# Attention scores on one core: the 64-row products of four heads gathered behind the 128-row ones

## The chip, the cores and the metric

The kernel runs on one core of one Trainium2 chip. The metric is the device time of one execution in microseconds (us). Before the change it is 2775.07 us, the median of three runs (2773.48 to 2775.38).

## What is computed

The program is two transformer-like blocks, one after the other, for 256 tokens of width 2048 in float32. The first block is gated linear attention, a short convolution and a feed-forward layer; the second a pooling mixer and an attention layer with a shared latent for keys and values. The change lies in this last attention layer. It has 16 heads. A head's query and key have 192 entries, 128 of them without and 64 with a rotary position code. Queries come in blocks of 128, and a block sees the keys up to its own end, that is 128 keys for block 0 and 256 for block 1:

```python
QBLOCK, N_HEADS, QK_NOPE, QK_ROPE, QK_HEAD = 128, 16, 128, 64, 192

def chunk_causal_attention(q, k, v):
    S = q.shape[1]
    scale = QK_HEAD ** -0.5
    outs = []
    for i in range(S // QBLOCK):
        q0, k_end = i * QBLOCK, (i + 1) * QBLOCK
        s = jnp.einsum('bqhd,bkhd->bhqk', q[:, q0:k_end], k[:, :k_end],
                       preferred_element_type=jnp.float32) * scale
        q_chunk = (q0 + jnp.arange(QBLOCK)) // CHUNK
        k_chunk = jnp.arange(k_end) // CHUNK
        mask = k_chunk[None, :] <= q_chunk[:, None]
        s = jnp.where(mask[None, None], s, -1e30)
        p = jax.nn.softmax(s, axis=-1).astype(v.dtype)
        outs.append(jnp.einsum('bhqk,bkhd->bqhd', p, v[:, :k_end]))
    return jnp.concatenate(outs, axis=1)
```

The score of a head is therefore a sum over 192 entries, which the kernel forms as a product over 128 rows plus a product over 64 rows.

## The kernel before, in words

Nearly all of the time goes into products of activations with weights from device memory. A weight block of 1 MB is loaded by SyncE into a tile `raw`, and each half of it, a unit, is split into a high part `wh` (ScalarE, line 268) and a low part `wl` (VectorE, line 269), so that fast float32 products can add up to nearly full precision. There are three `raw` tiles and four pairs of `wh` and `wl`; a unit is split up to three units ahead of its use (`ensure`, lines 254 to 274). TensorE goes through the units in the order of `weight_order` (line 58).

The other work is written as generators. At the end of each unit (`end_unit`, line 324) every generator whose time has come is advanced to its next `yield`, unless the planned cost of VectorE or ScalarE is too far ahead of that of TensorE. The planned cost of a product is booked in `mm` (line 227), which also issues it. So the order of each engine's instructions is fixed when the program is built, and attention is spread between the units of the last weights (`MLA`, line 48).

The attention of four heads is one generator, `attend(hq)` (line 1306), four in all. Its parts in order:

- For each of the two blocks of queries (line 1325): take a `main` tile of PSUM with four places of 256 columns, one a head, and write the four heads' scores into it (lines 1329 to 1335). `qn` and `kn` hold the 128 entries without position code on 128 rows; `qr` and `krp` hold the 64 entries with it, and there two heads share a tile: the even head lies on rows 0 to 63, the odd one on rows 64 to 127 (`bs`, line 1332). `HEAD_AT = (0, 2, 1, 3)` says which head a place c has, so places 0 and 1 hold even heads and places 2 and 3 odd ones. A `start` flag at c = 0 and at c = 2 clears two places at a time; the other products accumulate.
- ScalarE copies the scores to `s` (line 1339), GpSimd writes -1e30 over the masked corner (line 1341).
- VectorE takes maxima (line 1349), ScalarE the exponentials (line 1359), VectorE divides by the sums (lines 1364 to 1367).
- TensorE transposes the probabilities (line 1374, twelve groups of four in all), ScalarE copies them to `pt`, and TensorE multiplies them with the values `v` (lines 1386 and 1387).

Everything in the score products is plain float32. Such a product appears in the trace as two passes, each a weight load (PEld) and a MATMUL (PE). A 64-row product is a pass of the form 64*128, a 128-row one of 128*128; with one block of queries it has 128 columns, with the other 256. There are 8 score blocks in the kernel (4 groups of heads, 2 blocks of queries), each with 4 products of either height.

Of the kernel before, what the change touches and what calls it, by code (L numbers as in the profile page):

```python
# [99 lines left out]
def kernel(  # L100
# [48 lines left out]
    def slot(name, shape=(P, 4, T), dt=F32):  # L149
        return Slot(spool, big_places, "slot", shape, dt, name)  # L150
# [22 lines left out]
    def psum_later(kind, shape):  # L173
        while len(psum_places[kind]) < (1 + state["spare"] if kind == "main" else 1):
            yield 1
        return Psum(kind, shape)
# [8 lines left out]
    def elems(a):  # L185
        return math.prod(a.shape[1:])
# [21 lines left out]
    def ts(out, a, s1, s2, op0, op1=None):  # L208
        vec_cost(out, 2.0)
        if op1 is None:  # L210
            nc.vector.tensor_scalar(out, a, s1, None, op0)
        else:
            nc.vector.tensor_scalar(out, a, s1, s2, op0, op1)
# [9 lines left out]
    def act(out, a, f, scale=1.0, bias=0.0, **kw):  # L223
        spent["ACT"] += elems(out) / 1.2 + 100
        nc.scalar.activation(out, a, f, bias=bias, scale=scale, **kw)  # L225

    def mm(out, lhsT, rhs, start, stop):
        n = elems(rhs)
        spent["PE"] += (n / 2.4 if rhs.dtype == F32R else max(n / 0.6, 214.0)) + 2
        nc.tensor.matmul(out, lhsT, rhs, start=start, stop=stop, skip_group_check=True)  # L230
# [188 lines left out]
    def group_tok(name, g, rhs, kbs=range(NKB)):  # L419

        ps = psum_now("main", (P, 2, 512))
        kbs = list(kbs)
        for i, kb in enumerate(kbs):
            for half in range(2):
                wh, wl = next_unit(name, g, kb)
                x = rhs(i)[half]
                for j in range(2):
                    first = i == 0 and half + j == 0
                    last = i == len(kbs) - 1 and half + j == 2
                    for t in range(2):  # L430
                        tk = slice(t * P, (t + 1) * P)
                        mm(ps[:, t, :], x[:, j, 0, tk], wh[:, j, :], first, False)
                        mm(ps[:, t, :], x[:, j, 0, tk], wl[:, j, :], False, False)
                        mm(ps[:, t, :], x[:, j, 1, tk], wh[:, j, :], False, last)
                end_unit()
        return ps
# [99 lines left out]
    def small(name, shape):  # L536
        return const.tile(list(shape), F32, name=uid(name))

    def rstd_steps(out, m, mean_plus_eps):

        mean_plus_eps()
        act(out, m, AF.Sqrt)
        yield 1
        recip(out, out)
        mul(m, m, out)
        mul(m, m, out)
        ts(m, m, -0.5, 1.5, ALU.mult, ALU.add)
        mul(out, out, m)
# [281 lines left out]
    for g in range(4):  # L830
        ps = group_tok("v", g, h)
# [4 lines left out]
    for g in range(4):  # L836
        hold = {}
        ps = group("cc", g, h)
# [6 lines left out]
        ps = group("cx", g, h)  # L845
# [19 lines left out]
        ps = group("cb", g, h)  # L865
# [12 lines left out]
    for g in range(4):  # L878
        ps = group("gb", g, h)
        gt = {}  # L880
        spawn(gate_steps(ps, get("R"), AF.Sigmoid, gt, 0))
        ps = group("conv_out", g, cbu)
# [11 lines left out]
    for g in range(4):  # L894
        ps = group("r", g, h)
# [15 lines left out]
    for g in range(4):  # L911
        ps = group("ga", g, h)
# [4 lines left out]
        ps = group("gla_out", g, op)  # L917
# [24 lines left out]
    def residual(g):  # L942
        def into(ps, fs):
            for part in range(2):
                add(xs[g][:, fs, :], ps[:, :, part, :], xs[g][:, fs, :])

        return into
# [77 lines left out]
    for part in range(4):  # L1025
# [5 lines left out]
        for g in range(4):  # L1031
            ps = group("down", g, hid, range(4 * part, 4 * part + 4), residual(g))
# [49 lines left out]
    for half in range(2):  # L1082
        y = Pair(4)
        for gi in (2 * half, 2 * half + 1):
            pooled = Pair(2)
            for n in range(2):
                ps = group("u", 2 * gi + n, hp)
# [5 lines left out]
            for n in range(2):  # L1093
                ps = group("pgate", 2 * gi + n, hp)
# [3 lines left out]
            for n in range(2):  # L1098
                ps = group("pgroup", 2 * gi + n, pooled, range(2))
# [15 lines left out]
        for g in range(4):  # L1115
            ps = group("pout", g, y, range(4 * half, 4 * half + 4), residual(g))
# [98 lines left out]
    kn, krp, vq = [None] * 4, [None] * 2, []  # L1215
# [45 lines left out]
    qn, qr, qr2 = [None] * 4, [None] * 2, [None] * 2  # L1261
# [43 lines left out]
    HEAD_AT = (0, 2, 1, 3)  # L1305
    def attend(hq):
        while None in (qn[hq], kn[hq], qr[hq // 2], krp[hq // 2]):
            yield 1
        while hq and (hq - 1 not in begun or state["unit"] < begun[hq - 1] + STAGGER):
            yield 1  # L1310
        while len(big_places) < 6:
            yield 1
        begun[hq] = state["unit"]

        rq = rows["Cq"]
        hs = slice(4 * hq, 4 * hq + 4)
        a, b = qss[:, :, hs], qsc[:, :, hs]
        for t in range(2):
            r = rq[:, t:t + 1]
            ts(qss[:, t, hs], qss[:, t, hs], r, r, ALU.mult, ALU.mult)  # L1320
        yield from rstd_steps(b, a, lambda: ts(a, a, 1.0 / QK_HEAD, EPS, ALU.mult, ALU.add))
        for t in range(2):
            ts(qsc[:, t, hs], qsc[:, t, hs], rq[:, t:t + 1], QK_HEAD**-0.5, ALU.mult, ALU.mult)
        probs, mxs = [], []
        for blk in range(2):
            w = P * (blk + 1)
            ps = yield from psum_later("main", (P, 4, T))
            qsl = slice(blk * P, (blk + 1) * P)
            for c in range(4):
                i = HEAD_AT[c]  # L1330
                hd = 4 * hq + i
                bs = slice(64 * (hd % 2), 64 * (hd % 2) + 64)
                jr = hd // 2
                mm(ps[:, c, 0:w], qn[hq][:, i, qsl], kn[hq][:, i, 0:w], c % 2 == 0, False)
                mm(ps[:, c, 0:w], qr[jr // 4][bs, jr % 4, qsl], krp[jr // 4][bs, jr % 4, 0:w], False, True)
            yield 1
            s = slot("s")
            probs.append(s)
            act(s[:, :, 0:w], ps[:, :, 0:w], AF.Copy)
            ps.done()  # L1340
            nc.gpsimd.memset(s[0:64, :, w - 64:w], -1e30)
        qn[hq].free()
        kn[hq].free()
        yield 1
        for blk in range(2):
            w = P * (blk + 1)
            mx = small("mx", (P, 3, 4))
            mxs.append(mx)
            nc.vector.reduce_max(mx[:, 0, :], probs[blk][:, :, 0:w], axis=AX.X)
            stt(mx[:, 0, :].rearrange("p (b a) -> p b a", b=2), mx[:, 0, :].rearrange("p (b a) -> p b a", b=2),  # L1350
                -1.0, qsc[:, blk, hs].rearrange("p (a b) -> p b a", b=2), ALU.mult, ALU.mult)
        yield 1
        for blk in range(2):
            w = P * (blk + 1)
            mx = mxs[blk]
            for c in range(4):
                hd = 4 * hq + HEAD_AT[c]
                sv = probs[blk][:, c, 0:w]
                act(sv, sv, AF.Exp, scale=qsc[:, blk, hd:hd + 1], bias=mx[:, 0, c:c + 1],
                    accum_out=mx[:, 1, c:c + 1])  # L1360
        yield 2
        for blk in range(2):
            w = P * (blk + 1)
            nc.vector.reciprocal(mxs[blk][:, 2, :], mxs[blk][:, 1, :])
            for c in range(4):
                sv = probs[blk][:, c, 0:w]
                ts(sv, sv, mxs[blk][:, 2, c:c + 1], None, ALU.mult)
        yield 2
        pt0, pt1 = slot("pt0"), slot("pt1", (P, 4, P))
        for src, sc, dst in ((probs[0], slice(0, P), pt0[:, :, 0:P]), (probs[1], slice(0, P), pt0[:, :, P:T]),  # L1370
                             (probs[1], slice(P, T), pt1.t)):
            ps = yield from psum_later("misc", (P, 4, P))
            for c in range(4):
                nc.tensor.transpose(ps[:, HEAD_AT[c], :], src[:, c, sc], ident)  # L1374
            yield 1
            act(dst, ps.t, AF.Copy)
            ps.done()
        for s in probs:
            s.free()
        yield 2  # L1380
        while len(vq) <= hq:
            yield 1
        po = yield from psum_later("main", (P, 4, T))
        for i in range(4):
            isl = slice(i * P, (i + 1) * P)
            mm(po[:, i, :], vq[hq][:, 0, isl], pt0[:, i, :], i % 2 == 0, False)
            mm(po[:, i, P:T], vq[hq][:, 1, isl], pt1[:, i, :], False, True)
        vq[hq].free()
        pt0.free()
        pt1.free()  # L1390
        yield 1
        o = slot("oraw")
        act(o.t, po.t, AF.Copy)
        po.done()
        while hq not in gates:
            yield 1
        yield 1
        mul(o.t, o.t, gates[hq].t)
        gates[hq].free()
        ob.put(hq, o.t)  # L1400
        o.free()

    for g in range(4):
        spawn(attend(g))
    uses = {"bgate": hb, "kvb_k": cl, "kvb_v": cl, "qb_r": ql, "qb_n": ql}
    for i, (name, g) in enumerate(MLA):
# [8 lines left out]
        else:  # L1415
            ps = group_tok(name, g, cl, [0])
# [134 lines left out]
```

## Time and profile before

| what | value |
|---|---|
| median of three runs | 2775.07 us |
| the profiled execution's own time | 2773.71 us |
| its span, first to last instruction | 2771.9 us |
| TensorE busy | 2759.3 us |
| VectorE busy | 1787.4 us |
| ScalarE busy | 1346.4 us |
| DMA, mean rate | 185 GB/s |
| first score block starts | 2560.46 us |
| last score product starts | 2628.9 us |

The span is counted from the first instruction. Busy times are those of the engine's own work; weight loads are counted apart from products and overlap them. The ends of products are modelled by the profile, so the distance between starts is the safer measure of a product's cost.

### The profile page before, as it was taken

The numbers are of one execution on the slowest core, as the hardware profiler recorded it, in microseconds if no ns is written. First come the engines' busy times: TensorE is split into PE (matmuls) and PEld (weight loads), VectorE is DVE, ScalarE is ACT, GpSimd is POOL, SyncE is SP. The second block draws the span as 40 slices with busy tenths as digits, with TensorE's granted clock in tenths as the row PEclk, the third lists the DMA queues.
The fourth block names the chain that finished last, engine by engine and source line by source line (L and its number), as shares of the span: only waits on it lengthen the run. The fifth ranks groups of instructions, "written<-read, shape, count | busy, mean of one in ns | idle before, by whom it ended". The sixth has DMA issues, their size and how long they took to land.

```text
span 2771.9 us, 38593 instructions
## 1 busy us (share of the span) xinstructions
PE 2759.3 (100%) x15906; PEld 2403.6 (87%) x15906; DVE 1787.4 (64%) x2119; ACT 1346.4 (49%) x1584; POOL 25.7 (1%) x36
## 2 busy tenths in 40 slices
PE   8999999999999999999999999999999999999999
PEld 7888888888888888888888888888888888899788
DVE  6676666655665666656556566687657677768464
ACT  5644444444554444434444345554434445555563
POOL 0000000000000000000000000000000000000000
PEclk9999999999999999999999999999999999999999
DMA  6444455555555655555555555555555555555244
GB/s 250 175 149 155 167 182 183 194 186 189 191 182 198 214 193 186 185 195 183 194 185 191 189 185 195 190 185 195 185 193 185 186 194 199 201 181 183 92 171 148
DMA packets 73712, 511.69 MB, mean 185 GB/s; under 512 B 8208, under 2 KB 8752, under 8 KB 13248
## 3 DMA queue, kind: packets, MB, share of 16 engines
q1 hardware_dynamic: 72496, 506.94, 51.9%
q8 instruction: 124, 2.03, 0.3%
q10 hardware_dynamic: 1040, 2.29, 0.2%
q14 instruction: 52, 0.43, 0.0%
HBM read 504.99 MB, written 4.21 MB: 184 GB/s over the span
## 4 chain that ended last, share of the span: by engine, by line
PE 99%; DVE 0%; DMA 0%; ACT 0%; issue 0%; SPq 0%; DVEq 0%; ACTq 0%
PE main L230 96%; PE misc L230 2%; DMA raw<-w_q_dram 0%; PE misc L1374 0%; DVE wl L193 0%; DVE cum L683 0%; ACT e L225 0%; ACT wh L225 0%; SPq L246 0%; ACT ls L225 0%; DVE x L193 0%; ACT L225 0%; DVE ls L206 0%; DVE out L193 0%; PE misc L1241 0%
## 5 line engine op out<-in xcount | busy, mean ns | idle before, releaser
L230 PE MATMUL main<-part,wh 128*128 128x512 f32 (+1 forms) x7360 | 2278.5, 392 | 6.9 <-ACT wh L225 6.9
L193 DVE TENSOR_TENSOR wl<-raw,wh 128x1024 fp32r<-128x1024 f32 (+1 forms) x946 | 1152.2, 1221 | 937.8 <-ACT wh L225 929.7
L230 PEld LDWEIGHTS main<-part,wl 128*128 128x128 f32 x7200 | 1354.4, 188 | 314.4 <-DVE wl L193 1.8
L225 ACT ACTIVATE wh<-raw 128x1024 fp32r<-128x1024 f32 (+1 forms) x946 | 997.3, 1058 | 1193.9 <-PE main L230 1100.1
L230 PE MATMUL main<-part,wl 128*128 128x256 f32 x7200 | 1430.2, 278 | 0.7 <-DVE wl L193 0.5
L230 PEld LDWEIGHTS main<-part,wh 128*128 128x128 f32 x7360 | 1124.0, 189 | 11.4 <-ACT wh L225 7.1
L193 DVE TENSOR_TENSOR out<-main,out 128x512 f32<-128x512 f32 x164 | 112.0, 684 | 8.3 <-ACT out L225 8.3
L230 PE MATMUL main<-wh,part 128*128 128x512 f32 x320 | 105.3, 400 | 0.0
L225 ACT ACTIVATE out<-main 128x512 f32<-128x512 f32 x164 | 94.6, 577 | 0.0
L193 DVE TENSOR_TENSOR x<-main,x 128x512 f32<-128x512 f32 x128 | 88.0, 688 | 9.9 <-PE main L230 7.7
L230 PEld LDWEIGHTS main<-wh,part 128*128 128x128 f32 x320 | 60.8, 190 | 12.8 <-issue 0.3
L230 PE MATMUL main<-wl,part 128*128 128x512 f32 x160 | 63.0, 394 | 0.0
L225 ACT ACTIVATE part<-out 128x512 fp32r<-128x512 f32 x56 | 33.2, 626 | 50.7 <-DVE out L206 44.2
L193 DVE TENSOR_TENSOR out<-out,R 128x1024 f32<-128x1024 f32 x42 | 51.4, 1225 | 1.3
L225 ACT ACTIVATE Z<-Z 128x1024 f32<-128x1024 f32 x16 | 17.0, 1061 | 42.0 <-DVE Z L193 36.9
L193 DVE TENSOR_TENSOR part<-out,part 128x512 fp32r<-128x512 f32 x56 | 36.2, 687 | 0.5
L230 PEld LDWEIGHTS main<-wl,part 128*128 128x128 f32 x160 | 30.6, 191 | 5.8
L225 ACT ACT_TABLE_LOAD x24 | 30.8, 1283 | 1.1 <-PEq L1540 0.7
L206 DVE SCALAR_TENSOR_TENSOR part<-x,vec,part 128x256 fp32r<-128x256 f32 x64 | 26.8, 478 | 5.3 <-ACT part L225 5.3
L1068 POOL COPY s<-out 128x4 f32<-128x4 f32 x8 | 9.5, 1187 | 2208.2 <-ACT wh L225 1809.7
L230 PEld LDWEIGHTS misc<-Z 128*128 128x128 f32 x240 | 29.0, 191 | 1.0
L230 PE MATMUL misc<-Z 128*128 128x64 f32 (+1 forms) x240 | 28.6, 271 | 0.0
(188 smaller groups left out, 824.4 us busy)
## 6 DMA issues: line engine op xcount, KB each, us to landing
raw<-w_up_dram SPq DMA_DIRECT2D x64, 1024.0 KB, 4.8
raw<-w_down_dram SPq DMA_DIRECT2D x64, 1024.0 KB, 4.8
raw<-w_u_dram SPq DMA_DIRECT2D x32, 1024.0 KB, 4.8
raw<-w_pgate_dram SPq DMA_DIRECT2D x32, 1024.0 KB, 4.8
raw<-w_pout_dram SPq DMA_DIRECT2D x32, 1024.0 KB, 4.8
raw<-w_v_dram SPq DMA_DIRECT2D x16, 1024.0 KB, 4.9
raw<-w_cc_dram SPq DMA_DIRECT2D x16, 1024.0 KB, 4.8
raw<-w_cx_dram SPq DMA_DIRECT2D x16, 1024.0 KB, 4.8
```

Source lines behind the costliest of these rows:

```text
L193: nc.vector.tensor_tensor(out, a, b, op)
L206: nc.vector.scalar_tensor_tensor(out, a, s, b, op0, op1)
L225: nc.scalar.activation(out, a, f, bias=bias, scale=scale, **kw)
L230: nc.tensor.matmul(out, lhsT, rhs, start=start, stop=stop, skip_group_check=True)
L1068: nc.gpsimd.tensor_copy(nx[:, :, 0:d], cur[:, :, 0:d])
```

## The change

Inside a block of queries the loop over the four places is split in two. The first loop issues the four 128-row products in the order of the places. The second issues the four 64-row products, in the order of places 0, 2, 1, 3, that is on rows 0 to 63, 64 to 127, 0 to 63, 64 to 127. Every product keeps its operands, its place and its flags.

```diff
             qsl = slice(blk * P, (blk + 1) * P)
             for c in range(4):
                 i = HEAD_AT[c]
-                hd = 4 * hq + i
+                mm(ps[:, c, 0:w], qn[hq][:, i, qsl], kn[hq][:, i, 0:w], c % 2 == 0, False)
+            for c in (0, 2, 1, 3):
+                hd = 4 * hq + HEAD_AT[c]
                 bs = slice(64 * (hd % 2), 64 * (hd % 2) + 64)
                 jr = hd // 2
-                mm(ps[:, c, 0:w], qn[hq][:, i, qsl], kn[hq][:, i, 0:w], c % 2 == 0, False)
                 mm(ps[:, c, 0:w], qr[jr // 4][bs, jr % 4, qsl], krp[jr // 4][bs, jr % 4, 0:w], False, True)
             yield 1
             s = slot("s")
```

## Rows read from the trace of the kernel before

**Rows 1.** The page: busy time and share by engine, and the chain that ended last.
```profile
PE 2759.3 (100%) x15906; PEld 2403.6 (87%) x15906; DVE 1787.4 (64%) x2119; ACT 1346.4 (49%) x1584; POOL 25.7 (1%) x36
...
PE 99%; DVE 0%; DMA 0%; ACT 0%; issue 0%; SPq 0%; DVEq 0%; ACTq 0%
```

**Rows 2.** Waits, 2555 to 2772 us: waiter, waited for, total us, times, longest.
```profile
DVE wl L193 <- ACT wh L225: 75.4, 46, 5.4
ACT wh L225 <- PE main L230: 50.4, 31, 3.3
...
PEld main L230 <- issue: 10.3, 31, 0.3
```

**Rows 3.** Timeline of PE, first score block: start us, duration us, work, passes merged.
```profile
2560.46 0.38 PE L230 MATMUL main<-kn,qn 128*128 128x128 f32 x2
2560.77 0.49 PE L230 MATMUL main<-krp,qr 64*128 64x128 f32 x2
2561.18 0.49 PE L230 MATMUL main<-kn,qn 128*128 128x128 f32 x2
...
2563.68 1.95 PE L230 MATMUL misc<-ones,sq 128*128 128x1 f32 x16
2565.49 0.49 PE L230 MATMUL main<-wh,part 128*128 128x512 f32 x1
```

**Rows 4.** Timeline of PE, second score block.
```profile
2572.67 0.59 PE L230 MATMUL main<-kn,qn 128*128 128x256 f32 x2
2573.19 0.70 PE L230 MATMUL main<-krp,qr 64*128 64x256 f32 x2
2573.82 0.70 PE L230 MATMUL main<-kn,qn 128*128 128x256 f32 x2
...
2577.58 0.38 PE L230 MATMUL misc<-ones,sq 128*128 128x1 f32 x2
```

**Rows 5.** The chain near 2617 us (start, us), then timeline of PE, value product.
```profile
2617.43 0.44 PE misc L1374 x4
...
2641.66 2.78 PE L230 MATMUL main<-pt,v 128*128 128x256 f32 x16
2644.28 0.60 PE L1374 MATMUL misc<-cm,s 128*128 128x128 f32 x4
```

**Rows 6.** All instructions that read krp: count, ns min/median/max, first and last start, forms.
```profile
L230 PEld LDWEIGHTS main<-krp,qr x64: 182/184/186, 2560.8 to 2628.7; 64*128 64x128 f32 x64
L230 PE MATMUL main<-krp,qr x64: 272/374/480, 2560.8 to 2628.9; 64*128 64x128 f32 x32, 64*128 64x256 f32 x32
```

**Rows 7.** Timeline, chain, and windows (us, engines' busy, granted clock, DMA share, GB/s).
```profile
2558.64 0.39 PE L230 MATMUL main<-wl,part 128*128 128x512 f32 x1
2559.32 0.39 PE L230 MATMUL main<-wl,part 128*128 128x512 f32 x1
...
2567.41 0.63 PE L230 MATMUL main<-wl,part 128*128 128x512 f32 x1
2568.69 0.63 PE L230 MATMUL main<-wl,part 128*128 128x512 f32 x1
...
2553.34 1.68 PE misc L230 x16
...
2567.00:2570.40 3.40, 3.40 (x10) 2.63 (x9) 0.00 (x0) 0.62 (x1) 0.00 (x0) 0.50 0.50 212
2580.60:2584.00 3.40, 3.40 (x12) 2.94 (x12) 0.00 (x0) 0.48 (x1) 0.00 (x0) 0.50 0.02 5
```

**Rows 8.** Timeline of VectorE's divided probabilities and of PE's transposes.
```profile
2639.49 1.14 DVE L211 TENSOR_SCALAR s<-s,mx 128x256 f32<-128x256 f32 x4
2649.17 1.14 DVE L211 TENSOR_SCALAR s<-s,mx 128x256 f32<-128x256 f32 x4
...
2647.52 0.60 PE L1374 MATMUL misc<-cm,s 128*128 128x128 f32 x4
2656.61 1.04 PE L1374 MATMUL misc<-cm,s 128*128 128x128 f32 x8
```

## The prediction

> **What bounds the kernel now.** I began with the page's busy shares and its chain of waits [rows 1]: TensorE is busy for 2759.3 of 2771.9 us and the chain that ends last runs on it for 99%. So a microsecond taken from TensorE's own stream is a microsecond of the kernel, as long as nothing else becomes late. Then the view of waits, for the stretch from the first score block to the end [rows 2]: no row has TensorE's products waiting for ScalarE, VectorE or a transfer. ScalarE, which makes the weights' high halves, instead waits 50.4 us for TensorE to free buffers; the producers run ahead. The 10.3 us under "issue" is a weight load starting late with nothing released, 31 times at up to 0.3 us: TensorE holding itself up.
>
> The timeline shows where. In the first score block (128 keys) the 128-row products (kn,qn) and the 64-row ones (krp,qr) alternate, two passes each [rows 3]. The seven pairs from 2560.77 to 2563.68 take 0.416 us each; the block lasts from 2560.46 to 2563.68, 3.22 us. In the second block (256 keys) the seven pairs from 2573.19 to 2577.58 take 0.627 us each and the block lasts 4.91 us [rows 4]. Compare f32 passes that follow each other without a change of height: four 128-column transposes advance the chain by 0.44 us, 0.11 us a pass, and sixteen passes of the value product, eight of 256 columns and eight of 128, take 2.62 us up to the next start [rows 5], which leaves (2.62 - 8 x 0.11) / 8 = 0.217 us for a pass of 256. So a pair should take 0.22 or 0.434 us and takes 0.416 or 0.627: **each change between 128 and 64 rows costs 0.195 us**, the same at either width. That is the shape of a fixed pause (finish the old products, then load weights in the open), not of slower streaming. It adds up: 16 x 0.11 + 7 x 0.195 = 3.13 of the 3.22 us, and 16 x 0.217 + 7 x 0.195 = 4.84 of the 4.91; the rest belongs to the change at the block's end, which stays.
>
> **The change, part by part.** Nothing is added or removed: the same 64 + 64 passes, the same operands, no DMA, no wait. No instruction of another engine moves, and the queues of SyncE and GpSimd are not touched. The planner's estimate for a block is the same sum of the same calls, so the order around it stays.
>
> *Changes of height.* A block has eight now: seven inside it and one at its end. With the four 128-row products first there are two, one inside and one at the end. Six go, in each of 4 x 2 = 8 blocks (the 64-row products have 32 passes of either width [rows 6], eight to a block): 48 x 0.195 = **9.4 us**. Both widths pay the same, so no split is needed. All of it lies on TensorE's stream.
>
> *Changes of half.* The 64-row products now follow each other on rows 0 to 63, 64 to 127, 0 to 63, 64 to 127: three changes of half in a block, 24 in all. The trace of before has no such neighbours, so the price is bounded. Upper end: as dear as a change of height, 24 x 0.195 = 4.7 us given back. Lower end: the two halves run beside each other, and at each change one pass hides behind the one before. With 256 columns that hides 0.217 us three times in four blocks, 2.6 us. With 128 columns it need not hide anything: sixteen one-column passes take 2565.49 - 2563.68 = 1.81 us, 0.113 each [rows 3], so 0.11 us is what a weight load takes with nothing to stream; if loads overlap too it is up to 3 x 4 x 0.11 = 1.3 us more. Value taken: **0**, by the nearest rows: a new set of weights at unchanged height costs nothing beyond the pass [rows 5].
>
> The Trainium skill, "TensorEngine Tiling (Array Packing)", section "Key Properties", says that changing the tiling mode drains TensorE while changing merely the tile does not, and that different tiles can load and multiply in parallel. By that the halves would overlap and the sum would take the lower end, some 2.6 us more gained; the trace agrees with the drain (0.195 us a change of height) and has no row for the overlap.
>
> *The clock.* Twice in this stretch the granted clock is 0.50 (1.2 of 2.4 GHz) for 3.4 us [rows 7]. Three products take 2568.69 - 2567.41 = 1.28 us there against 2559.32 - 2558.64 = 0.68 us at full clock, 0.2 us more each; some eight fall in a stretch, so it costs 1.6 us. Both stretches come right after a score block followed by sixteen one-column products. One-column products alone did not do it: those at 2553.34 follow dense work, and no half clock comes after them. After the change the block is denser but the one-column run and its drain stay: it lies between the two rows. Ends: both stretches go (-3.2 us), both stay (0), two others come (+3.2). I take **one gone, 1.6 us**.
>
> *What waits on the blocks.* ScalarE copies the scores after the block's last product, as now, only earlier. The closest reader of what follows is the transposes: the last four heads' probabilities are written until 2649.17 + 1.14 = 2650.31, and their transposes are the second half of the eight that start at 2656.61 [rows 8], over 6 us later. For the four heads before, two shortened blocks (2 x 6 x 0.195 = 2.3 us) lie between scores and transposes, and theirs are written until 2639.49 + 1.14 = 2640.63 for a transpose at 2647.52, 6.9 us on. So I charge nothing; were that cover gone, the transposes would be late next and up to the 9.4 us would come back.
>
> **Sum** against the profiled execution (2773.7 us, of which the span is 2771.9): 9.4 + 0 + 1.6 = 11.0, giving 2762.7. That execution is 1.4 us below the median of the runs, 2775.07; so I forecast **2764.1 us** against the median.
>
> **Rivals.**
> - *The halves overlap.* For it: the two use other rows, and places of the output that alternate between 0, 1 and 2, 3, so no product accumulates where its neighbour does. Against: a product is two f32 passes in order, so only one pass in two has a partner, and no row shows two products at once. It is the outcome by the Trainium skill's "TensorEngine Tiling (Array Packing)", "Key Properties". 9.4 + 2.6 + 1.6 = 13.6: 2761.5 us, and down to 2758.6 with the 128-column gain and both clock stretches gone.
> - *A change of half pauses like a change of height*, in whole or in part. For it: the pause is what a half's first pass shows now. Against: second passes on the same half show none. In whole 9.4 - 4.7 + 1.6 = 6.3: 2768.8 us; with no help from the clock 2770.4; at half the pause 2766.4.
> - *Slower.* A change of half costs more than any change seen, because the second half's products wait for the first's to leave the array and then load both passes' weights in the open. It decides from (9.4 + 5.5) / 24 = 0.62 us a change, over three times the 0.195. At 0.7 us: 16.8 - 9.4 = 7.4 lost, 2782.5 us. Nothing in the rows reaches that.
> - *Given back downstream.* Scores come sooner, ScalarE and VectorE don't, and TensorE stands at the transposes. Against: the 6 us above, and ScalarE waiting for TensorE now. At worst 2775 us.
> - *The change does not do what it says*: 128-row products side by side pause as well. Against it are the transposes and value products, side by side without pauses. 2775 us.
>
> **How the numbers follow.** Forecast 0.40; overlap 0.34; pause at the half 0.15; slower 0.04; given back 0.04; nothing done 0.03. The range 2759.0 to 2769.5 holds the forecast, nearly all of the overlap case and most of the pause case, with either end of the clock term; what is left out is under 2 in 10. No change means within 0.2% of 2775.07, 5.5 us, about what a measurement of this kernel can tell. Faster by more is 0.40 + 0.34 + two thirds of 0.15 = 0.84, and 0.01 of a partial giving back: 0.85. Slower 0.04. The rest, 0.11, is no change.
>
> **What would show it.** In the timeline of the changed kernel the four 128-row products of a block start 0.22 us apart (0.434 in the wide block), then comes one pause, then 64-row products at the same pitch: a narrow block of 3.22 - 1.17 = 2.05 us and a wide one of 3.74. Overlap would show as 64-row passes starting closer than 0.217 us in the wide block, and 3.1 us for it. A pause at the half would show as starts 0.2 us late at every second 64-row pass and a block of 2.6 and 4.3 us. The 0.50 clock should appear once in this stretch. A wait of the transposes' weight loads for VectorE would prove the giving back. A narrow block above 2.7 us would prove the forecast wrong.

## The result and the profile after

The changed kernel takes 2758.28 us (median of four runs, 2756.16 to 2760.01) where the kernel before took 2775.23 us beside it: a ratio of 0.9939, interval 0.9924 to 0.9955. That is 17.0 us saved where 11.0 were forecast, and 0.7 us below the range. The direction was right; a term of the sum that had been put at nothing was a gain.

The page of the changed kernel still has TensorE as the bound; the lines answer to [rows 1]:

```profile
PE 2745.0 (100%) x15906; PEld 2399.1 (87%) x15906; DVE 1787.0 (65%) x2119; ACT 1346.1 (49%) x1584; POOL 25.7 (1%) x36
...
PE 98%; ACT 1%; DVE 0%; DMA 0%; issue 0%; SPq 0%; DVEq 0%; ACTq 0%
```

ScalarE has come into the chain with 1%, which is taken up below. The timeline of TensorE's products in the changed kernel, first and second score block, answers to [rows 3] and [rows 4] (start us, us, work, passes merged):

```profile
2562.26 1.05 PE L230 MATMUL main<-kn,qn 128*128 128x128 f32 x8
2563.24 0.72 PE L230 MATMUL main<-krp,qr 64*128 64x128 f32 x8
2563.88 1.95 PE L230 MATMUL misc<-ones,sq 128*128 128x1 f32 x16
...
2572.90 1.89 PE L230 MATMUL main<-kn,qn 128*128 128x256 f32 x8
2574.71 1.14 PE L230 MATMUL main<-krp,qr 64*128 64x256 f32 x8
2575.78 1.95 PE L230 MATMUL misc<-ones,sq 128*128 128x1 f32 x16
```

The narrow block takes 2563.88 - 2562.26 = 1.62 us instead of 3.22, the wide one 2575.78 - 2572.90 = 2.88 instead of 4.91. The 128-row products do as forecast: from 2572.90 to 2574.71, 1.81 us, are eight passes at 0.216 and the first part of the one pause. The 64-row products do not. Eight passes of 256 columns at 0.217 us would fill 1.74 us; here the eight and the pause behind them take 2575.78 - 2574.71 = 1.07 us. The passes must have run beside each other: in the trace the eight start in four pairs, the two of a pair less than 0.01 us apart. So did their weight loads (timeline of weight loads, changed kernel):

```profile
2563.24 0.52 PEld L230 LDWEIGHTS main<-krp,qr 64*128 64x128 f32 x8
```

Eight loads in 0.52 us, each of which lasts 0.18 us [rows 6] and which at the 0.11 us of a pass [rows 5] would start over a span of 0.77 us and end after 0.95.

Over all eight blocks, from the first start to the next work, the time goes from 4 x (3.23 + 4.92) = 32.6 us to 4 x (1.63 + 2.885) = 18.06 us: 14.5 us.

### The profile page after: what moved, and what is told of

It reads as the page before. It is cut to its first block, busy times and chain, and to the rows that moved or that the text cites. A ratio compares the mean times of both kernels' runs of the same rounds, so it can differ in the third digit from the quotient of the medians.

```text
span 2758.2 us, 38593 instructions
## 1 busy us (share of the span) xinstructions
PE 2745.0 (100%) x15906; PEld 2399.1 (87%) x15906; DVE 1787.0 (65%) x2119; ACT 1346.1 (49%) x1584; POOL 25.7 (1%) x36
## 4 chain that ended last, share of the span: by engine, by line
PE 98%; ACT 1%; DVE 0%; DMA 0%; issue 0%; SPq 0%; DVEq 0%; ACTq 0%
PE main L230 95%; PE misc L230 2%; DMA raw<-w_q_dram 0%; ACT s L225 0%; ACT wh L225 0%; ACT L225 0%; DVE wl L193 0%; PE misc L1375 0%; DVE cum L683 0%; ACT e L225 0%; SPq L246 0%; ACT pt L225 0%; ACT ls L225 0%; ACT out L225 0%; DVE x L193 0%
## 5 line engine op out<-in xcount | busy, mean ns | idle before, releaser
L225 ACT ACTIVATE part<-x,vec 128x256 fp32r<-128x256 f32 x64 | 27.2, 495 | 2.9 <-DMA x<-xT 2.8
```

## The experiments

Seven other kernels were run, and the changed one once more. In each diff `-` is the changed kernel, unless said otherwise. Times without a profile line are medians of the runs; the kernel before took 2774.83 us beside the first four and 2774.98 us beside the last four.

**All 64-row products on one half.** This keeps the gathering and takes away what the two halves can do for each other. It leaves out the odd heads' own position part, for which it takes the rows of the even heads.

```diff
-                bs = slice(64 * (hd % 2), 64 * (hd % 2) + 64)
+                bs = slice(0, 64)
```

> All four 64-row products of a block read rows 0 to 63, so the odd heads' position part is computed from the even heads' rows; everything else is as after the change. Theory (the gain is 48 changes of height saved plus the two halves running beside each other): only the first part is left, no two 64-row passes start within 0.1 us of each other, the narrow block takes 2.05 us and the wide one 3.74 us (1.63 and 2.89 after the change), and the kernel is some 5.2 us slower than after the change, near 2763.5 us. Rival (the closeness of starts has nothing to do with the halves, any 64-row products pair up): blocks stay at 1.63 and 2.89 us and the time at 2758.

2762.78 us, a ratio of 0.9959 [0.9944, 0.9974] to the kernel before. Timeline of its products, first and second block, and of the weight loads of the first block's 64-row products:

```profile
2560.31 1.05 PE L230 MATMUL main<-kn,qn 128*128 128x128 f32 x8
2561.29 1.16 PE L230 MATMUL main<-krp,qr 64*128 64x128 f32 x8
2562.38 0.38 PE L230 MATMUL misc<-ones,sq 128*128 128x1 f32 x2
...
2569.77 1.89 PE L230 MATMUL main<-kn,qn 128*128 128x256 f32 x8
2571.59 1.99 PE L230 MATMUL main<-krp,qr 64*128 64x256 f32 x8
2573.51 0.27 PE L230 MATMUL misc<-ones,sq 128*128 128x1 f32 x1
...
2561.29 0.96 PEld L230 LDWEIGHTS main<-krp,qr 64*128 64x128 f32 x8
```

2.07 and 3.74 us a block, 4 x (2.07 + 3.74) = 23.24 us for all eight, and eight weight loads take 0.96 us instead of 0.52. So the six changes of height in each block are worth 32.6 - 23.24 = 9.4 us, and the two halves 23.24 - 18.06 = 5.2 us. The 128-row products are untouched: 0.98 us to the next group here as in the changed kernel. By the medians this kernel is 4.5 us slower than the changed one and not 5.2; 0.5 us of that is a wait for ScalarE, told below, that the changed kernel's trace has and this one has not.

**The order of the places.** Is the alternation needed?

```diff
-            for c in (0, 2, 1, 3):
+            for c in range(4):
```

> The 64-row products stay gathered but go in the order of the places: two products on rows 0 to 63, then two on rows 64 to 127. Theory A (each half works through its own products, and the queue looks past the other half's work): blocks as after the change, 1.63 and 2.89 us, time 2758 us. Theory B (passes start in program order, and only neighbours on different halves run together): one pair of passes overlaps instead of four, the narrow block takes about 1.94 us and the wide one about 3.52 us, time near 2762 us.

2758.05 us, 0.9938 [0.9922, 0.9955]. Timeline of its products:

```profile
2560.08 1.05 PE L230 MATMUL main<-kn,qn 128*128 128x128 f32 x8
2561.06 0.72 PE L230 MATMUL main<-krp,qr 64*128 64x128 f32 x8
2561.71 0.38 PE L230 MATMUL misc<-ones,sq 128*128 128x1 f32 x2
...
2570.73 1.89 PE L230 MATMUL main<-kn,qn 128*128 128x256 f32 x8
2572.55 1.14 PE L230 MATMUL main<-krp,qr 64*128 64x256 f32 x8
2573.62 0.27 PE L230 MATMUL misc<-ones,sq 128*128 128x1 f32 x1
```

1.63 and 2.89 us: the same blocks. Four passes on the lower half stand in the program ahead of the first on the upper half, and still all of them pair up, the two of a pair 0.013 us apart in the trace. Theory B, that passes start in program order, falls; each half works through its own products and does not wait for the other's turn. The alternating order, half of what the change writes, brings nothing by itself. What the gathering does is put work for both halves close together.

**Two smaller groups.** Two 128-row products, their two 64-row ones, and the same again (lines that are merely indented further are cut).

```diff
+            for cc in ((0, 2), (1, 3)):
-            for c in range(4):
+                for c in cc:
...
-            for c in (0, 2, 1, 3):
+                for c in cc:
```

> A block in two parts: two 128-row products, then their two 64-row ones on the two halves, then the same again. Two more changes of height per block than after the change. Theory: each costs 0.195 us and the overlap inside each part is kept, so the narrow block takes 2.02 us and the wide one 3.28 us, and the kernel is 8 x 0.39 = 3.1 us slower than after the change. Rival (the pause is paid once per gathered run of products whatever its length, or the overlap needs four products in a row): narrow 1.63 or 2.24 us, wide 2.89 or 3.7 us.

2760.67 us in its one run. Timeline of its products, first block:

```profile
2560.16 0.60 PE L230 MATMUL main<-kn,qn 128*128 128x128 f32 x4
2560.70 0.49 PE L230 MATMUL main<-krp,qr 64*128 64x128 f32 x4
2561.12 0.71 PE L230 MATMUL main<-kn,qn 128*128 128x128 f32 x4
2561.76 0.49 PE L230 MATMUL main<-krp,qr 64*128 64x128 f32 x4
2562.18 0.38 PE L230 MATMUL misc<-ones,sq 128*128 128x1 f32 x2
```

2.02 us for the block, 3.28 for the wide one (2571.18 to 2574.46), both as the theory has them: two more changes of height at 0.195 us, and two products on different halves suffice for the overlap. Eight blocks add up to 21.2 us, 3.1 more than after the change. The time is 2.4 us above the 2758.28 of the changed kernel; one run can't settle the difference, so the blocks are what decides here.

**Wider sums.** The clock term of the forecast rested on two stretches. Their cause is tried by giving the one-column products 64 equal columns, of which one is read:

```diff
-        pq = yield from psum_later("misc", (P, 2, 4))
+        pq = yield from psum_later("misc", (P, 2, 4, 64))
...
-                mm(pq[:, t, j:j + 1], sq[:, j, t * P:(t + 1) * P], one_col, t + j == 0, True)
+                mm(pq[:, t, j, :], sq[:, j, t * P:(t + 1) * P], one_cols, t + j == 0, True)
```

and the same for the keys (line 1229). `one_cols` are 64 columns of ones; the lines that define it and that read the sums are cut here.

> After the change, with the sixteen-pass runs of one-column products (the sums of squares of queries and keys in the last layer) given 64 equal columns instead of one; the same number of products and weight loads. Theory (the half clock behind a score block is called up by these runs, in which TensorE loads weights and streams almost nothing): the runs keep their 0.11 us a pass, no half clock stands between 2500 and 2640 us, and the kernel gains up to 1.6 us for each stretch that goes. Rival (it is the pauses of the score blocks): a half-clock stretch still follows a score block, and the time stays at 2758 us. Rival (a pass gets longer with its columns): each run of sixteen gets longer than 1.85 us.

2756.67 us, 0.9935 [0.992, 0.995]. The timeline shows a run of sums as long as before, 2565.80 - 2563.99 = 1.81 us, and the window from 2500 to 2640 us has full clock (busy of TensorE, weight load, VectorE, ScalarE, GpSimd; granted clock; DMA share, GB/s):

```profile
2563.99 2.00 PE L230 MATMUL misc<-ones,sq 128*128 128x64 f32 x16
2565.80 0.48 PE L230 MATMUL main<-wh,part 128*128 128x512 f32 x1
...
2500.00:2640.00 140.00, 139.72 (x909) 122.89 (x909) 99.00 (x192) 94.74 (x156) 2.44 (x8) 1.00 0.44 151
```

So 64 columns cost nothing over one, 0.113 us a pass with either; the weight load, which is the same in both, is what seems to set the pace. The profiled execution is the slowest of the four (2758.49 us), and its one stretch of half clock lies elsewhere, at the start of the kernel from 17.29 to 20.70 us. On the clock the run speaks for the theory but does not decide, since the intervals of the two kernels overlap.

**Wider sums in the kernel before.** The same edit, `-` being the kernel before.

> The kernel before, with the one-column sums given 64 columns. Theory (the thin runs behind a score block call up the half clock, and what the change gained beyond the shorter blocks was one or two such stretches that failed to come): no half clock between 2500 and 2640 us, score blocks as before (3.23 and 4.92 us), and 1.6 us gained for each of the up to two stretches, so 2771.6 to 2773.2 us where the kernel before takes 2774.8. Rival (the many pauses inside the alternating score blocks suffice): a half-clock stretch still comes and the time stays at 2774.8 us.

2770.53 us in ten runs, 0.9988 [0.9979, 0.9997]. Its windows row for 2500 to 2640 us, and below it that of the kernel before, where the two stretches of [rows 7] stand:

```profile
2500.00:2640.00 140.00, 140.00 (x821) 114.82 (x821) 89.73 (x170) 85.38 (x141) 2.50 (x8) 1.00 0.40 139
```

```profile
2500.00:2640.00 140.00, 140.00 (x805) 114.51 (x804) 89.02 (x168) 82.18 (x130) 2.50 (x8) 0.98 0.38 132
```

The score blocks are as long as before (3.23 and 4.92 us) and their pauses are all there, yet the half clock is gone and with it 2773.71 - 2770.54 = 3.2 us between the two profiled executions: 1.6 us a stretch, as priced. The rival, that the pauses suffice, falls. The time that was expected, 2771.6 to 2773.2 us, was missed all the same: the medians lie 4.5 us apart, more than two stretches; where the rest stands in the executions that were not profiled can't be seen.

**The gate's products on two parts of the array.** If parts of the array that share no rows are independent, it should show with 16 rows too. The decay gate of the first block has two groups of four 16-row products, and `lr` holds eight copies of its 16 rows already.

```diff
-        nc.scalar.dma_start(out=wg[0:16, :], in_=w_gate_up)
+        for b in (0, 64):
+            nc.scalar.dma_start(out=wg[b:b + 16, :], in_=w_gate_up)
...
-        mul(lr[0:16, :], lr[0:16, :], rows["R"][0:16, :])
+        mul(lr.t, lr.t, rows["R"].t)
...
-            for j in range(4):
-                n = 4 * hf + j
-                mm(z[:, j, :], wg[0:16, n * P:(n + 1) * P], lr[0:16, :], j % 2 == 0, True)
+            for j in (0, 2, 1, 3):
+                n, b = 4 * hf + j, 64 * (j // 2)
+                mm(z[:, j, :], wg[b:b + 16, n * P:(n + 1) * P], lr[b:b + 16, :], j % 2 == 0, True)
```

> After the change, with the 16-row products of the decay gate in the first block put on two places of the array: the gate's weights are loaded twice, to rows 0 to 15 and 64 to 79, and of each four products two use either. Theory (parts of the array that share no rows work through their own passes, whatever the number of rows): the eight passes of each of the two groups start in pairs, a group takes 1.07 us from its first start to the next work instead of 1.92 us, so 1.7 us in all, about 2756.6 us. Rival (only 64-row products run beside each other): pairs don't form, the groups stay at 1.92 us and the time at 2758.3.

2755.0 us, 0.9931 [0.9916, 0.9947]. Timeline of the first group, in this kernel and, below, in the changed one:

```profile
67.28 1.13 PE L230 MATMUL main<-lr,wg 16*128 16x256 f32 x8
68.34 0.50 PE L230 MATMUL main<-part,wh 128*128 128x512 f32 x1
```

```profile
68.61 1.99 PE L230 MATMUL main<-lr,wg 16*128 16x256 f32 x8
70.53 0.50 PE L230 MATMUL main<-part,wh 128*128 128x512 f32 x1
```

1.06 us instead of 1.92, the length that was worked out from the score blocks. Two groups save 1.7 us; the span is 1.3 us shorter than that of the changed kernel's second profile below (2753.6 against 2754.9), neither having a stretch of half clock. 0.3 us of the other 0.4 lies ahead of both groups: TensorE's first product starts 6.44 us after the first instruction in this execution and 6.12 us in the other, and over the ten profiles here that start varies from 5.91 to 6.97 us.

One condition stays untested. In every run with an overlap the two parts of the array also wrote to different places of the output, one part to places 0 and 1, the other to 2 and 3. The run on one half shows that different places alone are not enough; whether the overlap needs them, no run here can say.

**Both, and the changed kernel once more.** The first has both edits above.

> After the change, with the 64-column sums and the gate's products on two parts of the array. If both theories hold the gains add: up to 1.6 us for each half-clock stretch that goes, and 1.7 us, so 2754.5 to 2756 us, faster than before and than after the change. If either gives its gain back (a transfer that comes late at the start of the kernel, a stretch of half clock elsewhere), it stays at 2756.7 or above.

> The changed kernel once more, beside the others on one chip: 2758.3 us, score blocks of 1.63 and 2.89 us. Open is where its half-clock stretches lie: if they hang on chance alone there may be none to two of them behind the score blocks, and the time moves by 1.6 us with each.

With both: 2754.84 us, 0.993 [0.9917, 0.9943], its five runs from 2754.51 to 2755.22. The changed kernel beside it: 2757.94 us, 0.9942 [0.9929, 0.9955], from 2756.70 to 2760.22. By its median the kernel with both is the fastest of all here, 0.2 us ahead of the one with the gate alone, which is less than either one's runs differ, and its slowest run is ahead of the changed kernel's fastest of all nine (2756.16). The second profile of the changed kernel (2756.70 us) shows no stretch of half clock between its first 13 us and TensorE's last product, the first (2760.01) two stretches, one of them at the start of the kernel and one behind the first score block:

```profile
16.98:20.39 3.41, 3.41 (x12) 2.93 (x11) 1.59 (x3) 2.40 (x5) 0.00 (x0) 0.50 1.05 420
2566.74:2570.15 3.41, 3.41 (x10) 2.65 (x9) 0.24 (x2) 1.36 (x3) 0.00 (x0) 0.50 0.76 276
```

These are windows of the first profile. Two stretches at 1.6 us are the 3.3 us between the two executions. The blocks are 1.63 and 2.885 us in both, so a kernel's own time is best read from its blocks, and one or two stretches between single executions are no difference of the kernels.

## Why the prediction missed

**Right: what bounds, and the changes of height.** The bound is TensorE's stream and 48 changes of height went. The price of 9.4 us is what the run on one half shows, 32.6 - 23.24.

**Wrong: "Changes of half ... Value taken: 0".** This is the step that failed. The nearest rows said that new weights at unchanged height cost nothing beyond the pass, and those rows had one part of the array only, so they could not speak of two. Measured, the term is a gain of 5.2 us.

**Wrong too: its lower end.** The rival of overlapping halves had the right mechanism and was mis-sized: "a product is two f32 passes in order, so only one pass in two has a partner" gave 2.6 us, with 1.3 more if loads overlap. The plain order shows that passes of the two halves keep no common order: all eight passes pair, four of eight vanish, 4 x 0.216 in a wide and 4 x 0.11 in a narrow block, 4 x (0.86 + 0.44) = 5.2 us. That loads overlap as well is why the narrow block gains its share, where 0.11 us a load had seemed a floor. The range ended at 2759.0 because the most favourable case by this price, with both stretches of half clock gone, was 2758.6.

That the time fell outside the range took more than this step. With the overlap at its measured size, the 0.5 us given back (below) and the one stretch of half clock that was forecast, the time would have been 2775.07 - (9.4 + 5.2 - 0.5 + 1.6) = 2759.4 us, inside the range by luck, and the term of 0 would have been as wrong.

The Trainium skill, "TensorEngine Tiling (Array Packing)", "Key Properties", has tiles load and multiply in parallel, without any such limit, and the trace agrees: 0.52 us for eight loads. The Trainium skill's "TensorE: Matmul & The Clock Gate", section "Part 3: Packing small matmuls — row/col tiling", has products start in program order. The run with the plain order differs, and the measurement decides: passes on one half don't overlap (the run on one half), so for eight passes to fit into the time of four, the upper half's first pass must run beside the lower half's first, ahead of three passes that the program has before it.

**The clock: right in kind, small in size.** One stretch was taken to go, 1.6 us. Where neither execution has a stretch, the spans are 2768.8 us (wider sums in the kernel before) and 2754.9 us (changed kernel), 13.9 us apart. The medians are 17.0 us apart; the 3 us that remain would be two stretches fewer in a median run. The times speak for it without showing it: the ten runs of the wider sums in the kernel before lie near 2770.4, 2772.1 and 2773.9 us, one stretch apart, and by such steps the median run of the kernel before (2775.23) has three stretches and that of the changed kernel (2758.28) one.

What the forecast named as a sign, one 0.50 clock in this part of the kernel, is in the first profile of the changed kernel and not in the second. With 64 columns in the sums behind the score blocks the half clock behind them went away, in the kernel before. That denser blocks alone make it rarer is argued from counts, and not settled: behind the blocks the one profile of before has two stretches; of six profiles with gathered blocks and one-column sums four have one (the changed kernel's first, the plain order, one half, two groups) and two have none (its second, the gate's products).

**Right: little is given back, though something is.** 14.5 us less in the blocks is 13.9 less in the spans of the two executions without half clock. The view of waits of the changed kernel, from 2555 to 2758 us, has a row that [rows 2] has not:

```profile
PEld main L230 <- ACT v L225: 0.5, 1, 0.5
```

The timeline shows where, at 2630.95 us: the first product of the last gate's weights waits for ScalarE's copy of the third of the four value tiles, which holds a place in PSUM and is queued behind the last exponentials.

```profile
2629.08 0.58 ACT L225 ACTIVATE s<-s,mx,qsc 128x256 f32<-128x256 f32 x1
...
2629.67 1.24 ACT L225 ACTIVATE v<-main,Rl 128x512 f32<-128x512 f32 x2
...
2630.95 0.50 PE L230 MATMUL main<-part,wh 128*128 128x512 f32 x1 [0.28 <-ACT v L225]
```

This is the forecast's giving back, with ScalarE as its engine but not at the transposes: I had measured the slack of the transposes and not that of the PSUM places. The timeline of the kernel before has the same copy and the product behind it:

```profile
2643.18 1.24 ACT L225 ACTIVATE v<-main,Rl 128x512 f32<-128x512 f32 x2
...
2644.63 0.71 PE L230 MATMUL main<-part,wh 128*128 128x512 f32 x2
```

There the copy ends at 2644.42 us, only 0.2 us before that product. The wait explains 0.5 of the 0.6 us. It also brings ScalarE into the chain, from 2611.67 to 2630.91 us, which is the 1% of the page: 19 us of chain, but a cost of only the 0.5 us by which it ended late, since TensorE had work of its own until then.

The rivals "slower" and "does not do what it says" are out: the 128-row products ran at 0.11 and 0.216 us a pass. So is a pause at the change of half, by which the blocks would have taken 2.6 and 4.3 us.

The sum with the measured terms is 14.5 from the blocks less 0.5, 14.0 us. The other 3 of the 17.0 us are put down to the clock as what remains.

## What to carry to other kernels

Gather products that use few rows, on parts of the array that share no rows, and keep them away from full-height ones: here each change of height cost 0.195 us and each pass with a partner on another part was free, weight load included, in both orders that were tried (with the outputs in different places, as above). An operation that no trace shows is not priced by its nearest neighbour where a rule says that it belongs to another kind: bound it by the best that the rule allows. And see whether one-column products can be given more columns: here 64 took the time of one, and in the three profiles with them no half clock stood behind the score blocks.

## What was not expected of the hardware

- The two halves of the array don't share an order: with four passes for the lower half ahead of four for the upper one, the block took 1.63 us, as with alternating products.
- Weight loads of the two halves run beside each other as well, eight in 0.52 us where eight on one half take 0.96.
- Sixteen f32 passes of 64 columns take the 1.81 us that sixteen of one column take.
